# Two more slots for weight chunks and a coarser spread of the first norm's conditioning, in a hybrid decoder step

## The chip, the cores and the metric

The kernel runs on one core of one Trainium2 chip. The metric is the device time in microseconds (us) of one execution. The core has a matrix engine (TensorE, PE in the rows), VectorE (DVE), ScalarE (ACT), GpSimd (POOL) and SyncE (SP), whose queue issues nearly all loads from the chip's main memory (HBM). Each engine works through its own list of instructions in order. Where one needs another's result, it waits for a semaphore.

## The reference, cut to what matters

One decoder layer is computed for 256 prompt tokens and 8 x 4 sample tokens, 288 columns in all, in float32. Every norm is modulated by a conditioning vector `c` (one for the prompt, one for each of 8 samples).

```python
mod = silu(c) @ w_ada + b_ada                       # 2048 -> 6 * 2048
sh1, sc1, g1, sh2, sc2, g2 = split(mod, 6)
h = rmsnorm(x, norm1) * (1 + sc1) + sh1             # first norm, conditioned
proj = h @ w_in                                     # pool, z, x/B/C, dt
...                                                 # pooling mixer, Mamba-2 mixer
x = x + g1 * (mix @ w_out)
h2 = rmsnorm(x, norm2) * (1 + sc2) + sh2
...                                                 # gated MLP with a causal convolution
x = x + g2 * (act @ w_down)
```

The change touches how `sh1` and `sc1`, the conditioning of the first norm, are computed beside `h @ w_in`.

## The kernel before

Every activation lies with features on the 128 partitions and the 288 tokens along the row. A weight chunk is 128 x 1024 floats (512 KB). It is loaded by SP into a slot with the tag `raw`, and `split` (lines 214 to 219) makes two float32r parts of it: a copy on ACT (`whi`) and the rest on DVE (`wlo`). The activation is split likewise (`h1h`, `h1l`). `mm3` (lines 221 to 225) then issues three matmuls of 288 columns for each 128 x 128 tile: high x high, high x low, low x high. These make up the main stream of PE, from the input projection (`xbc`, `mm_uz`) over `mm_out` to `mm_gate`, `mm_val` and `mm_down`.

The conditioning is another kind of matmul. `ada_mm` (lines 249 to 254) puts the 9 conditioning vectors, padded to 32 columns, on PE as the stationary side and streams plain float32 weight columns. Four such matmuls, one for each 32 columns of the array, stand side by side; we call four that belong together a quad. The profile writes each of these matmuls as two records. `ada_group_units(gi)` makes `sh1` and `sc1` for one group of feature tiles. `KGROUPS` divides the 16 feature tiles into groups of 1, 1, 2, 4, 4 and 4. `ada_part_units` makes the other four parts of `mod` later, as `adap2` to `adap5`.

The input projection starts before all conditioning is known. For each group `gi`, `xbc_units(gi)` goes over 28 output tiles (`ET` = 28), multiplies by the group's feature tiles alone and adds into `cvp`, `upp`, `ups` or `zy`. Beside it the loop at lines 846 to 870 steps a generator for the conditioning of the next group: one step per output tile from the tile number `NX[gi]` on. At tile 24 (`ET - 4`) the generator is drained, and `modulate` makes the next group's `h1h` and `h1l`. A step of a group of four loads one chunk, which holds one quad; a step of a group of two holds two quads. A step loads its chunk, then yields, and issues the matmuls at the next step. There are 16 steps of a group of four, 8 of the group of two.

The slots: the class `_W` hands out `RAW1` = 8 slots in turn in the first half of the kernel, and one more (`RAW2`) from the output projection on. SP's list is in order, so a load whose slot is not free holds up all loads behind it. GpSimd issues some small transfers itself (software DMA); their descriptors lie in a scratch area in SBUF.

The order of instructions on each engine is not that of the Python code alone. A scheduler places the instructions when the program is built, by program order and by when it believes operands to be ready. So a quad may be broken: one of its matmuls stands before some matmuls of the main stream, three behind.

Of the kernel before, what the change touches and what calls it, by code (L numbers as in the profile page):

```python
# [19 lines left out]
KT = D // P  # L20
# [15 lines left out]
ET = XT + len(UEARLY) + 3 * ZEARLY  # L36
EPS = 1e-6
WU = (14, 2, 2, 2, 6)
RAW1, RAW2 = 8, 1
SPLIT1, SPLIT2 = 2, 2  # L40
YK = 2
NX = (10, 1, 1, 1, 1)
AY = 2

RA1, RA2, RB1, RB2, RB3 = 0.5, 0.4, 1.0, 1.0, 1.0
# [86 lines left out]
def kernel(ctx: ExitStack, tc, ins, outs):  # L132
    nc = tc.nc
# [28 lines left out]
    ada = kp.tile([P, 6, KT, NC9], F32, name="ada")  # L162
# [45 lines left out]
    def load(key):  # L208
        off, cols = S.items[key]
        t = wp[0].tile([P, RAWC], F32, tag="raw", name="raw_" + "_".join(map(str, key)))  # L210
        nc.sync.dma_start(t[:, :cols], wflat[off:off + P * cols].rearrange("(p n) -> p n", p=P))
        return t
# [59 lines left out]
    def ada_group_units(gi):  # L272

        k0, gk = KGROUPS[gi]
        nj = min(2 * gk, 4)
        nb = 2 * gk * P // nj
        per = RAWC // (nj * nb)
        ps = pa.tile([P, 512], F32, tag="ada", name=f"adag{gi}")
        for q in range(KT // per):
            raw = load(("ada", gi, q))  # L280
            yield
            if gk == 1:

                for kk in range(0, per, 2):
                    k = q * per + kk
                    for j in range(4):
                        nc.tensor.matmul(ps[32 * j:32 * j + 32, :nb], sc_c[:, k + j // 2, :],
                                         raw[:, kk * 256 + j * P:kk * 256 + j * P + P],
                                         start=(k == 0), stop=(k == KT - 2), tile_position=(0, 32 * j))
                if gi == 0 and q < WU[3]:  # L290
                    warm_pe(WU[2], raw[:, 0:P])
                continue
            for kk in range(per):
                ada_mm(ps, raw, q * per + kk, kk * nj * nb, nb, range(nj))
        r = 32 * nj
        if gk == 1:
            asb = ada_sb(ps, nb, f"g{gi}")
            pt = aux(f"adat_g{gi}")
            nc.tensor.matmul(pt[:, :r], asb[:, :nb], early[:, K_S2:K_S2 + r], start=True, stop=True)
            if gi == 0:  # L300
                warm_pe(WU[4], asb[:, 0:P])
        else:
            pt = ada_tr(ada_sb(ps, nb, f"g{gi}", r), nb, f"g{gi}", r)
        for i in range(nb // P):

            o = ada[:, 0:2, k0:k0 + gk, :].rearrange("p a (b i) c -> p a b i c", b=nj // 2)[:, :, :, i, :]
            b = bada[:, 0:2, k0:k0 + gk].rearrange("p a (b i) -> p a b i", b=nj // 2)[:, :, :, i]
            src = pt[:, i * r:(i + 1) * r].rearrange("p (a b c) -> p a b c", a=2, b=nj // 2)[:, :, :, 0:NC9]
            nc.vector.tensor_tensor(o, src, b.unsqueeze(3).to_broadcast([P, 2, nj // 2, NC9]), ALU.add)
        ada_scale(0, 1, early[:, V_N1:V_N1 + KT], k0, gk)  # L310
# [535 lines left out]
    for gi in range(len(KGROUPS)):  # L846
        last = gi + 1 == len(KGROUPS)
        if last:
            hi, lo = split(load(("dt",)), 0, KT * NH, "dt")
            ps = pm.tile([P, 512], F32, tag="mm", name="mm_dt")  # L850
# [3 lines left out]
        else:  # L854
# [5 lines left out]
            k0, gk = KGROUPS[gi + 1]  # L860
        for i, m in enumerate(xbc_units(gi)):
            if not last:
                if i >= NX[gi]:
                    next(nxt, None)
                if i == ET - 4:
                    drain(nxt)
                    modulate(xav(k0, gk), rstd1, 0, 0, k0, gk, f"g{gi + 1}")
            else:
                pull(back, 0.5 if m < 20 else RB1) if m >= 9 else None
                pull(adas, RA1 / AY)  # L870

# [360 lines left out]

# [27 lines left out]
```

## Time and profile before

| what | us |
| --- | --- |
| device time, median of 3 runs | 1394.89 |
| the three runs | 1394.83, 1396.73, 1394.89 |
| device time of the profiled execution | 1395.98 |
| its span, first to last instruction | 1394.2 |
| PE busy | 1374.9 |
| DVE busy | 822.3 |
| ACT busy | 577.0 |
| POOL busy | 259.8 |

The profiled execution lies 1.1 us above the median, and 1.8 us of it lie outside the span. A busy PE is not a PE that does as much as it can: matmuls overlap in its pipeline, and the records last longer than the distance between their starts. Such a stream is better read by the distance from one start to the next.

### The profile page before, as it was taken

The page shows a single profiled execution, that of the slowest core. Times are in us where ns is not written, and L with a number is a line of the kernel's source. Part 1 is how long each engine was busy: PE and PEld are TensorE (multiplying, and loading weights), DVE is VectorE, ACT ScalarE, POOL GpSimd, SP SyncE. Part 2 cuts the span into 40 slices and gives each one's busy share as a digit, 9 for nine tenths or more (in the row PEclk, how much of TensorE's full clock was granted, in tenths as well). Part 3 has the DMA queues.
Part 4 walks back from the last instruction along what each step waited for, and adds up shares of the span by engine and source line. Part 5 has one row for each costly group of instructions (what it writes and reads, how often), then busy time and mean ns, then how long its engine had stood idle before and what let it go on. Part 6 is the DMA issues. An engine that isn't in the chain of part 4 may idle for free.

```text
span 1394.2 us, 26416 instructions
## 1 busy us (share of the span) xinstructions
PE 1374.9 (99%) x10565; PEld 1253.5 (90%) x10565; DVE 822.3 (59%) x1409; ACT 577.0 (41%) x925; POOL 259.8 (19%) x466
## 2 busy tenths in 40 slices
PE   8999999999999999999999999999999999999997
PEld 7777888776668998989999999999999999999997
DVE  3775666867465446845665445666664466666553
ACT  5322333466673334533443333444343344444452
POOL 0000000344332222211211000221220011122221
PEclk9999999999999999999999999999999999999999
DMA  8889886867869886688655555655555555555631
GB/s 339 313 318 316 294 287 248 338 248 289 321 228 354 319 313 244 215 287 296 210 185 181 164 172 181 207 184 186 176 180 169 180 190 189 192 188 193 194 118 68
DMA packets 97196, 323.20 MB, mean 232 GB/s; under 512 B 10737, under 2 KB 19889, under 8 KB 97073
## 3 DMA queue, kind: packets, MB, share of 16 engines
q1 hardware_dynamic: 93168, 310.63, 64.8%
q0 software_dynamic: 3184, 9.69, 2.0%
q8 instruction: 83, 1.36, 0.4%
q10 hardware_dynamic: 720, 1.19, 0.2%
q14 instruction: 41, 0.33, 0.1%
HBM read 309.78 MB, written 10.39 MB: 230 GB/s over the span
## 4 chain that ended last, share of the span: by engine, by line
PE 70%; DVE 1%; issue 0%; ACT 0%; POOL 0%; DVEq 0%; POOLq 0%; ACTq 0%
PE mm_down L223 7%; PE mm_down L225 7%; PE mm_down L224 7%; PE mm_gate L225 6%; PE mm_gate L223 6%; PE mm_val L224 6%; PE mm_gate L224 6%; PE mm_val L225 6%; PE mm_val L223 6%; PE mm_out L223 3%; PE mm_out L224 2%; PE mm_out L225 2%; PE adap L252 2%; PE mm_up L223 1%; PE mm_up L224 1%; PE mm_up L225 1%
## 5 line engine op out<-in xcount | busy, mean ns | idle before, releaser
L223 PE MATMUL mm_down<-ah,whi_down 128*128 128x288 f32 x688 | 203.7, 296 | 0.0
L225 PE MATMUL mm_down<-ah,wlo_down 128*128 128x288 f32 x688 | 203.5, 296 | 0.0
L224 PE MATMUL mm_down<-al,whi_down 128*128 128x288 f32 x688 | 203.3, 295 | 0.0
L225 PE MATMUL mm_gate<-h2h,wlo_gate 128*128 128x288 f32 x640 | 190.2, 297 | 0.0
L223 PE MATMUL mm_gate<-h2h,whi_gate 128*128 128x288 f32 x640 | 189.8, 297 | 0.0
L224 PE MATMUL mm_gate<-h2l,whi_gate 128*128 128x288 f32 x640 | 189.3, 296 | 0.0
L224 PE MATMUL mm_val<-h2l,whi_val 128*128 128x288 f32 x640 | 188.8, 295 | 0.0
L225 PE MATMUL mm_val<-h2h,wlo_val 128*128 128x288 f32 x640 | 188.5, 295 | 0.0
L223 PE MATMUL mm_val<-h2h,whi_val 128*128 128x288 f32 x640 | 188.0, 294 | 0.0
L218 DVE TENSOR_TENSOR wlo_gate<-raw_gate,whi_gate 128x1024 fp32r<-128x1024 f32 x80 | 98.4, 1232 | 140.5 <-ACT whi_gate L217 140.3
L218 DVE TENSOR_TENSOR wlo_down<-raw_down,whi_down 128x1024 fp32r<-128x1024 f32 x96 | 108.2, 1127 | 116.0 <-ACT whi_down L217 115.1
L217 ACT CAST whi_down<-raw_down 128x1024 fp32r<-128x1024 f32 x96 | 92.2, 961 | 168.8 <-PE mm_down L224 120.3
L217 ACT CAST whi_gate<-raw_gate 128x1024 fp32r<-128x1024 f32 x80 | 83.8, 1050 | 168.3 <-PE mm_gate L224 76.2
L223 PE MATMUL xbc<-h1h,whi_xbc 128*128 128x288 f32 x448 | 139.1, 312 | 2.4 <-ACT h1h L350 1.3
L217 ACT CAST whi_val<-raw_val 128x1024 fp32r<-128x1024 f32 x80 | 84.1, 1051 | 127.8 <-issue 101.0
L224 PE MATMUL xbc<-h1l,whi_xbc 128*128 128x288 f32 x448 | 132.2, 296 | 0.0
L225 PE MATMUL xbc<-h1h,wlo_xbc 128*128 128x288 f32 x448 | 130.5, 298 | 0.6 <-DVE wlo_xbc L218 0.5
L224 PEld LDWEIGHTS mm_down<-al,whi_down 128*128 128x128 f32 x688 | 129.7, 189 | 0.0
L225 PEld LDWEIGHTS mm_down<-ah,wlo_down 128*128 128x128 f32 x688 | 129.6, 188 | 0.0
L223 PEld LDWEIGHTS mm_down<-ah,whi_down 128*128 128x128 f32 x688 | 129.6, 188 | 0.0
L223 PEld LDWEIGHTS mm_gate<-h2h,whi_gate 128*128 128x128 f32 x640 | 120.4, 188 | 5.0 <-ACT ah L1025 4.2
L224 PEld LDWEIGHTS mm_gate<-h2l,whi_gate 128*128 128x128 f32 x640 | 120.6, 189 | 0.0
(321 smaller groups left out, 3043.1 us busy)
## 6 DMA issues: line engine op xcount, KB each, us to landing
raw_adap<-wflat SPq DMA_DIRECT2D x128, 512.0 KB, 4.9
raw_gate<-wflat SPq DMA_DIRECT2D x80, 512.0 KB, 3.7
raw_val<-wflat SPq DMA_DIRECT2D x80, 512.0 KB, 3.5
raw_ada<-wflat SPq DMA_DIRECT2D x64, 512.0 KB, 5.5
raw_xbc<-wflat SPq DMA_DIRECT2D x55, 512.0 KB, 5.9
raw_down<-wflat SPq DMA_DIRECT2D x48, 512.0 KB, 3.6
raw_out<-wflat SPq DMA_DIRECT2D x32, 512.0 KB, 7.0
raw_down<-wflat SPq DMA_DIRECT2D x32, 384.0 KB, 3.1
```

The lines of the kernel that those rows point to most:

```text
L217: nc.scalar.copy(hi[:, :n], raw[:, a:a + n])
L218: nc.vector.tensor_tensor(lo[:, :n], raw[:, a:a + n], hi[:, :n].bitcast(F32), ALU.subtract)
L223: nc.tensor.matmul(ps, whi[:, w], bh, start=first, stop=False)
L224: nc.tensor.matmul(ps, whi[:, w], bl, start=False, stop=False)
L225: nc.tensor.matmul(ps, wlo[:, w], bh, start=False, stop=last)
L252: nc.tensor.matmul(ps[32 * j:32 * j + 32, :nb], sc_c[:, k, :], raw[:, c:c + nb], start=(k == 0), stop=(k == KT - 1), tile_position=(0, 32 ...
```

## The change

Four edits:

- `RAW1` goes from 8 to 10: two more slots of 4 KB a partition for weight chunks.
- The scratch for software-DMA descriptors is set to 8192 bytes, half of the default, which makes room for the two slots.
- In the loop, the generator for a group of two or four is stepped at every third output tile (`AE` = 3) instead of at every one. For the second group of one nothing changes.
- In `ada_group_units`, a step of a group of four loads two chunks and issues two quads (`AG` = 2).

```diff
--- before.py
+++ after.py
@@ -36,10 +36,11 @@
 ET = XT + len(UEARLY) + 3 * ZEARLY
 EPS = 1e-6
 WU = (14, 2, 2, 2, 6)
-RAW1, RAW2 = 8, 1
+RAW1, RAW2 = 10, 1
 SPLIT1, SPLIT2 = 2, 2
 YK = 2
 NX = (10, 1, 1, 1, 1)
+AG, AE = 2, 3
 AY = 2
 
 RA1, RA2, RB1, RB2, RB3 = 0.5, 0.4, 1.0, 1.0, 1.0
@@ -276,10 +277,17 @@
         nb = 2 * gk * P // nj
         per = RAWC // (nj * nb)
         ps = pa.tile([P, 512], F32, tag="ada", name=f"adag{gi}")
-        for q in range(KT // per):
-            raw = load(("ada", gi, q))
+
+
+        at = AG if gk == 4 else 1
+        for q0 in range(0, KT // per, at):
+            raws = [load(("ada", gi, q)) for q in range(q0, q0 + at)]
             yield
-            if gk == 1:
+            for q, raw in zip(range(q0, q0 + at), raws):
+                if gk > 1:
+                    for kk in range(per):
+                        ada_mm(ps, raw, q * per + kk, kk * nj * nb, nb, range(nj))
+                    continue
 
                 for kk in range(0, per, 2):
                     k = q * per + kk
@@ -289,9 +297,6 @@
                                          start=(k == 0), stop=(k == KT - 2), tile_position=(0, 32 * j))
                 if gi == 0 and q < WU[3]:
                     warm_pe(WU[2], raw[:, 0:P])
-                continue
-            for kk in range(per):
-                ada_mm(ps, raw, q * per + kk, kk * nj * nb, nb, range(nj))
         r = 32 * nj
         if gk == 1:
             asb = ada_sb(ps, nb, f"g{gi}")
@@ -860,7 +865,7 @@
             k0, gk = KGROUPS[gi + 1]
         for i, m in enumerate(xbc_units(gi)):
             if not last:
-                if i >= NX[gi]:
+                if i >= NX[gi] and (gk == 1 or (i - NX[gi]) % AE == 0):
                     next(nxt, None)
                 if i == ET - 4:
                     drain(nxt)
@@ -1232,7 +1237,7 @@
 
 def kernel(**inputs):
     ins = _layout(inputs)
-    nc = _bacc.Bacc("TRN2", target_bir_lowering=False, num_devices=1)
+    nc = _bacc.Bacc("TRN2", target_bir_lowering=False, num_devices=1, dynamic_dma_scratch_size=8192)
     i = {n: nc.dram_tensor(n, a.shape, F32, kind="ExternalInput").ap() for n, a in ins.items()}
     o = {n: nc.dram_tensor(n, s, F32, kind="ExternalOutput").ap() for n, s in _OUTS.items()}
     with _tile.TileContext(nc) as tc:
```

The scheduler lays out the whole program anew. Three places show what becomes of the order. In the names, `adag2` and `adag4` are the accumulators of the conditioning of groups 2 and 4, `raw_ada_4_5` is chunk 5 for group 4, and `xbc3_10` is output tile 10 of the input projection with the features of group 3. The last number of a name is a buffer.

PE, in the projection with group 1, before. The conditioning of the group of two stands between output tiles, eight matmuls (two quads) at a time:

```order
L252 MATMUL adag2_534<-raw_ada_2_2_567,sc_c_79 32x128 x8
L223 MATMUL xbc1_5_585<-h1h1_172,whi_xbc1_0_518 128x288
L224 MATMUL xbc1_5_585<-h1l1_188,whi_xbc1_0_518 128x288
L225 MATMUL xbc1_5_585<-h1h1_172,wlo_xbc1_0_519 128x288
L252 MATMUL adag2_534<-raw_ada_2_3_583,sc_c_79 32x128 x8
L223 MATMUL xbc1_6_601<-h1h1_172,whi_xbc1_0_518 128x288
```

The same place after:

```order
L253 MATMUL adag2_534<-raw_ada_2_2_591,sc_c_79 32x128
L224 MATMUL xbc1_5_565<-h1h1_172,whi_xbc1_0_518 128x288
L225 MATMUL xbc1_5_565<-h1l1_188,whi_xbc1_0_518 128x288
L226 MATMUL xbc1_5_565<-h1h1_172,wlo_xbc1_0_519 128x288
L253 MATMUL adag2_534<-raw_ada_2_2_591,sc_c_79 32x128 x2
L224 MATMUL xbc1_6_571<-h1h1_172,whi_xbc1_0_518 128x288
L225 MATMUL xbc1_6_571<-h1l1_188,whi_xbc1_0_518 128x288
L226 MATMUL xbc1_6_571<-h1h1_172,wlo_xbc1_0_519 128x288
L253 MATMUL adag2_534<-raw_ada_2_2_591,sc_c_79 32x128 x2
L224 MATMUL xbc1_7_577<-h1h1_172,whi_xbc1_0_518 128x288
```

The eight matmuls of one chunk, which stood together, are now dealt out in runs of one, two, two and three, with an output tile between each.

PE, in the projection with group 3, before:

```order
L224 MATMUL xbc3_6_1349<-h1l7_194,whi_xbc3_3_1345 128x288
L225 MATMUL xbc3_6_1349<-h1h7_178,wlo_xbc3_3_1346 128x288
L252 MATMUL adag4_1244<-raw_ada_4_4_1341,sc_c_79 32x256 x4
L223 MATMUL xbc3_7_1370<-h1h4_175,whi_xbc3_3_1345 128x288
L224 MATMUL xbc3_7_1370<-h1l4_191,whi_xbc3_3_1345 128x288
L225 MATMUL xbc3_7_1370<-h1h4_175,wlo_xbc3_3_1346 128x288
```

The same chunk after:

```order
L225 MATMUL xbc3_10_1423<-h1l7_194,whi_xbc3_5_1419 128x288
L226 MATMUL xbc3_10_1423<-h1h7_178,wlo_xbc3_5_1420 128x288
L253 MATMUL adag4_1244<-raw_ada_4_4_1377,sc_c_79 32x256 x4
L253 MATMUL adag4_1244<-raw_ada_4_5_1379,sc_c_79 32x256 x4
L224 MATMUL xbc3_11_1450<-h1h4_175,whi_xbc3_5_1419 128x288
L225 MATMUL xbc3_11_1450<-h1l4_191,whi_xbc3_5_1419 128x288
L226 MATMUL xbc3_11_1450<-h1h4_175,wlo_xbc3_5_1420 128x288
```

Here the conditioning of a group of four stood alone between output tiles, one quad after each; now two quads stand together, after every third tile.

DVE, from the moment at which the conditioning of group 4 is known (`adat_g4`) to the modulated features of that group (`h1l8` and so on), before. It stands beside output tiles 18 to 20 of 28:

```order
L309 TENSOR_TENSOR ada_77<-adat_g4_1631,early_69 128x2x2x9 x2
L543 TENSOR_TENSOR cvp3_163<-cvp3_163,xbc3_18_1643 128x256
L267 SCALAR_TENSOR_TENSOR amul_78<-ada_77,early_69 128x36
L543 TENSOR_TENSOR cvp3_163<-cvp3_163,xbc3_18_1643 128x8x4
L342 TENSOR_SCALAR h_g4_1763<-h_g4_1763,amul_78,ada_77 128x256 x3
L543 TENSOR_TENSOR cvp3_163<-cvp3_163,xbc3_19_1658 128x256
L543 TENSOR_TENSOR cvp3_163<-cvp3_163,xbc3_19_1658 128x8x4
L342 TENSOR_SCALAR h_g4_1763<-h_g4_1763,amul_78,ada_77 128x256
L351 TENSOR_TENSOR h1l8_195<-h_g4_1763,h1h8_179 128x288
```

After. It stands beside output tiles 25 to 27 of 28, and `xbc4_0` is the first tile that uses these features:

```order
L314 TENSOR_TENSOR ada_77<-adat_g4_1757,early_69 128x2x2x9 x2
L268 SCALAR_TENSOR_TENSOR amul_78<-ada_77,early_69 128x36
L347 TENSOR_SCALAR h_g4_1763<-h_g4_1763,amul_78,ada_77 128x256 x4
L548 TENSOR_TENSOR zy1_208<-zy1_208,xbc3_25_1779 128x288
L356 TENSOR_TENSOR h1l8_195<-h_g4_1763,h1h8_179 128x288
L356 TENSOR_TENSOR h1l9_196<-h_g4_1763,h1h9_180 128x288
L356 TENSOR_TENSOR h1l10_197<-h_g4_1763,h1h10_181 128x288
L356 TENSOR_TENSOR h1l11_198<-h_g4_1763,h1h11_182 128x288
L548 TENSOR_TENSOR zy1_208<-zy1_208,xbc3_26_1799 128x288
L219 TENSOR_TENSOR wlo_xbc4_0_1840<-raw_xbc_4_0_1837,whi_xbc4_0_1839 128x1024
```

The chain started beside output tile 18 of 28 and now starts beside tile 25.

## Rows read from the trace of the kernel before

**Rows 1.** Page, part 1: busy us (share of the span) xinstructions, by engine.

```profile
PE 1374.9 (99%) x10565; PEld 1253.5 (90%) x10565; DVE 822.3 (59%) x1409; ACT 577.0 (41%) x925; POOL 259.8 (19%) x466
```

**Rows 2.** PE's waits, the two longest: us in total, times, longest.

```profile
PE mm_uz L225 <- DVE wlo_uz L218: 1.4, 1, 1.4
PE cse L682 <- DVE ada L327: 1.4, 1, 1.4
```

**Rows 3.** Timeline of PE (start, us, instruction, [idle before <- releaser]): two waits.

```profile
89.33 0.40 PE L225 MATMUL xbc<-h1h,wlo_xbc 128*128 128x288 f32 x1 [0.53 <-DVE wlo_xbc L218]
...
274.49 0.40 PE L223 MATMUL xbc<-h1h,whi_xbc 128*128 128x288 f32 x1 [0.93 <-ACT whi_xbc L217]
```

**Rows 4.** Waits of SP's queue: loads that waited for a slot behind conditioning.

```profile
SPq L211 <- PE adag L252: 75.0, 48, 5.5
```

**Rows 5.** Timeline of PE: one quad of a group of four, then the main stream.

```profile
107.37 0.29 PE L225 MATMUL xbc<-h1h,wlo_xbc 128*128 128x288 f32 x1
107.59 0.64 PE L252 MATMUL adag<-raw_ada,sc_c 128*32 128x256 f32 x8
...
108.40 0.30 PE L224 MATMUL xbc<-h1l,whi_xbc 128*128 128x288 f32 x1
108.53 0.29 PE L225 MATMUL xbc<-h1h,wlo_xbc 128*128 128x288 f32 x1
```

**Rows 6.** Timeline of PE: two quads in a row, group of four.

```profile
76.69 0.30 PE L225 MATMUL xbc<-h1h,wlo_xbc 128*128 128x288 f32 x1
76.92 1.07 PE L252 MATMUL adag<-raw_ada,sc_c 128*32 128x256 f32 x16
...
78.16 0.30 PE L224 MATMUL xbc<-h1l,whi_xbc 128*128 128x288 f32 x1
```

**Rows 7.** Timeline of PE: two quads of the group of two.

```profile
42.04 0.29 PE L225 MATMUL xbc<-h1h,wlo_xbc 128*128 128x288 f32 x1
42.27 0.64 PE L252 MATMUL adag<-raw_ada,sc_c 128*32 128x128 f32 x16
...
43.08 0.29 PE L224 MATMUL xbc<-h1l,whi_xbc 128*128 128x288 f32 x1
```

**Rows 8.** Timeline of PE: later parts, two quads, then a single matmul of one.

```profile
222.23 0.29 PE L225 MATMUL xbc<-h1h,wlo_xbc 128*128 128x288 f32 x1
222.45 1.92 PE L252 MATMUL adap<-raw_adap,sc_c 128*32 128x512 f32 x16
...
224.54 0.29 PE L224 MATMUL xbc<-h1l,whi_xbc 128*128 128x288 f32 x1
...
225.07 0.29 PE L224 MATMUL xbc<-h1l,whi_xbc 128*128 128x288 f32 x1
225.29 1.04 PE L252 MATMUL adap<-raw_adap,sc_c 128*32 128x512 f32 x2
...
226.51 0.29 PE L223 MATMUL xbc<-h1h,whi_xbc 128*128 128x288 f32 x1
```

**Rows 9.** Timelines of PE and DVE: from group 4's conditioning to its features.

```profile
137.31 0.38 PE L263 MATMUL adat_g<-early,asb_g 128*128 128x128 f32 x2
...
139.09 1.34 DVE L342 TENSOR_SCALAR h_g<-h_g,amul,ada 128x256 f32<-128x256 f32 x3
...
142.06 1.23 DVE L218 TENSOR_TENSOR wlo_xbc<-raw_xbc,whi_xbc 128x1024 fp32r<-128x1024 f32 x1 [0.42 <-ACT whi_xbc L217]
```

**Rows 10.** Timelines of DVE and POOL: modulation of groups 3 and 4.

```profile
94.84 1.56 DVE L351 TENSOR_TENSOR h1l<-h_g,h1h 128x288 fp32r<-128x288 f32 x4
...
88.19 1.36 POOL L347 TENSOR_TENSOR h_g<-h_g,amul 128x128 f32<-128x128 f32 x1 [37.26 <-DVE cvp L543]
...
139.19 0.58 POOL L347 TENSOR_TENSOR h_g<-h_g,amul 128x128 f32<-128x128 f32 x1 [48.08 <-DVE cvp L543]
```

**Rows 11.** POOL's software DMA: issues on its timeline; KB, us to landing.

```profile
870.58 2.01 POOL L1040 DMA_DIRECT2D sq<-sbx  x4 [2.59 <-DMA o_ssms<-hst]
sq<-sbx POOLq DMA_DIRECT2D x16, 64.0 KB, 4.1
```

## The prediction, made before the changed kernel had run

> **What bounds the kernel now.** First the page's first part: PE is busy for 1374.9 of 1394.2 us, DVE for 822.3, POOL for 259.8 [rows 1]. So the kernel can only become faster where PE does less or waits less. Second, what ended PE's waits: the two longest take 1.4 us each, and both are for DVE [rows 2]. Two more, in the input projection, are idle times of 0.53 us (for DVE's low half of a chunk) and 0.93 us (for ACT's high half) [rows 3]. No long wait of PE is for a load. SP, on the other hand, waited 75.0 us in 48 loads for a slot that conditioning still held [rows 4]; that is where ten slots help, but these waits are SP's, and PE pays for none of them. The first two edits therefore bring nothing on their own. They cost something only through what the scheduler makes of the order, and there I count.
>
> **The price of leaving the main stream.** Two neighbouring matmuls of the main stream start 0.13 us apart (108.40 and 108.53) [rows 5]. Around one quad of a group of four the distance is 108.40 − 107.37 = 1.03; two steps of the main stream are in it, so the quad cost 1.03 − 0.26 = 0.77 [rows 5]. Two quads in a row cost 78.16 − 76.69 − 0.26 = 1.21 [rows 6]. The difference, 0.44, is the quad itself; 0.77 − 0.44 = 0.33 is the departure: out of the main stream and back. For the group of two, two quads cost 43.08 − 42.04 − 0.26 = 0.78; less the departure 0.45, or 0.22 a quad [rows 7]. For the later parts two quads cost 224.54 − 222.23 − 0.26 = 2.05, so (2.05 − 0.33) / 2 = 0.86 a quad. One matmul alone of such a quad cost 226.51 − 225.07 − 0.26 = 1.18, which is 0.33 + 0.85 [rows 8]: a piece broken off costs as much as a whole quad, because the four run side by side. I count for each run of conditioning matmuls one departure, and one quad for each four begun.
>
> **The change, part by part.** The new order of PE gives the numbers.
>
> *Groups of four in pairs.* Before, the 16 quads of groups 4 and 5 stood mostly alone; now most stand in twos. Group 4 goes from 16 runs to 9, group 5 from 16 to 9, group 3 from 19 to 16: 17 departures fewer.
>
> *The group of two, dealt out.* Its chunks have only eight matmuls each, and the scheduler breaks them into pieces of two to five. Its runs go from 8 to 16, the quads begun from 17 to 21. Net of both, 68 runs of the first norm's conditioning become 59: −9 × 0.33 = −3.0. Quads begun: +4 × 0.22 = +0.9 for the group of two and +1 × 0.44 = +0.4 for the groups of four. Together −1.7 us.
>
> *Parts moved.* The diff does not name the later parts, but the scheduler lays them out anew: 48 runs become 53, 79 − 76 = 3 more quads are begun. +5 × 0.33 + 3 × 0.86 = +4.2. The low end is +1.7, if broken pieces overlapped their neighbours after all; Rows 8 speak against it, so I take 4.2. PE's work in sum: −1.7 + 4.2 = +2.5 us.
>
> There is a rule against counting in this way. A departure costs 0.33 us whatever is streamed in it [rows 5, 6]. The Trainium skill, page "TensorEngine Tiling (Array Packing)", section "Key Properties", says that a change of the tiling mode (not of the tile alone) drains the engine; the trace agrees that leaving costs something. By that rule by itself the number of departures would be the whole price; this is the third rival below.
>
> *Waits that go.* In the new order the low half that PE waited for at 89.33 stands earlier in DVE's list, and the high half of 274.49 stands ahead of the long ACT instruction that held it. The idle time counts from the recorded end of the last matmul; the records last 0.30, and 0.13 is the step, so 0.17 has to be added: 0.53 + 0.17 = 0.7 and 0.93 + 0.17 = 1.1 [rows 3, 5]. Together −1.8. The two waits of 1.4 [rows 2] stand between the same neighbours as before; I leave them.
>
> *Waits that come.* The last step of a generator now comes later, so the chain from conditioning to the next group's features starts close to that group. For group 4: from the PE matmul that makes `adat_g4` to the first modulation on DVE 139.09 − 137.31 = 1.8 us; four modulations at 1.34 / 3 each 1.8; two additions at about 0.4; four `h1l` 1.56; the first low half of `xbc4_0` 1.2 [rows 9, 10]. That makes 1.8 + 1.8 + 0.8 + 1.6 + 1.2 = 7.2, all in a row on DVE. PE in the same time has 36 steps of the main stream, 36 × 0.13 = 4.7, then five conditioning matmuls in one run, 0.33 + 2 × 0.44 = 1.2, and then needs that low half: 5.9. It waits 1.3. POOL's half of the modulation, which the high half on ACT needs, runs beside it. At the other three boundaries, PE has 22 to 33 steps and one or two runs; the same sum there ends near zero. Ends: 0, if the scheduler's distance is enough, and 0.8, if POOL's first multiplication takes 1.36 us as for group 3 and not 0.58 as for group 4 [rows 10]. I take the middle, 0.4 each. New waits: 1.3 + 3 × 0.4 = +2.5. Waiting on DVE there queues the additions of the output tiles behind the modulation; their PSUM buffers come free later, which is in the ends above.
>
> *Halved scratch.* It costs nothing as long as POOL's issues find room. The densest place is four issues in 2.01 us, each landing after 4.1 us [rows 11]. One bound is zero; the other is the fifth rival.
>
> **The sum** against the profiled execution's own time, 1395.98 (span 1394.2 and 1.8 around it): 1395.98 + 2.5 − 1.8 + 2.5 = 1399.2. That execution lies 1.1 above the median of the runs shown, so 1398.1.
>
> **Rivals.** *The chains fit.* DVE has slack, and the order was laid out to suit it. New waits 0: 1395.98 + 2.5 − 1.8 − 1.1 = 1395.6. For it: PE waits for little anywhere [rows 1, 2]. Against: the 7.2 us are a plain sum of rows.
>
> *PE gains, so faster.* If pieces overlap with their neighbours and the new layout also removes the two waits of 1.4 [rows 2]: −3.0 + 0.4 + 1.7 − 1.8 − 2.8 = −5.5, hence 1389.4. Against: the price of the broken piece [rows 8] and the unmoved neighbours.
>
> *Only departures count.* All runs of PE that leave the main stream go from 138 to 134. If pieces cost nothing besides: −4 × 0.33 = −1.3, with the same waits 1395.98 − 1.3 + 0.7 − 1.1 = 1394.3. That is no change.
>
> *Late at all four boundaries, slower.* POOL's two operations share each boundary with DVE's two-input subtractions. At 1.36 in place of 0.58, twice, each boundary is 1.6 later [rows 10]: 4 × 1.6 = 6.4 in place of 2.5. 1395.98 + 2.5 − 1.8 + 6.4 − 1.1 = 1402.0. It decides once POOL's half ends later than DVE's, which for group 3 it did.
>
> *The scratch fills.* If each of the four issues had to wait until the one before had landed, POOL would be held 3 × (4.1 − 0.5) = 10.8 us at each of four places [rows 11]. POOL also makes small copies for each feed-forward tile. PE is reached only beyond POOL's lead; half of it reaching PE gives 4 × 5.4 = 22, some 1420. The Trainium skill, page "DMA: Bandwidth & Descriptors", section "SWDGE vs HWDGE vs iDMA", says that the rings of these descriptors lie in a reserved part of SBUF; no run here shows how full it gets.
>
> **How the numbers follow.** About 0.2%, 2.8 us, is what a measurement of this kernel can tell from no change: 1392.1 to 1397.7. Forecast (1398.1, its own range 1396.3 to 1399.9) 0.38, of which 0.22 lie above the bound and 0.16 within. Chains fit 0.20, within. Only departures 0.12, within. Faster 0.12, of which 0.10 below the bound. Late everywhere 0.13 and scratch 0.05, above. So faster 0.10, same 0.16 + 0.20 + 0.12 + 0.02 = 0.50, slower 0.40. The range from 1393.5 to 1402.2 leaves out nearly all of the faster case and the scratch, and a tail of "late everywhere".
>
> **What the profile after would show.** If I am right: PE's departures around groups 4 and 5 cost 1.21 for two quads; the waits at 89 and 274 are gone; a wait of about 1.3 us for DVE's `wlo_xbc` stands at the start of the projection with group 4, and less than 0.8 at the other three; the parts have five more runs. The second rival shows in single part matmuls that cost 0.4 rather than 1.18; the fourth in POOL's modulation of 1.3 us and more at every boundary; the fifth in wide gaps between POOL's DMA issues. The prediction is wrong if PE waits for loads anywhere, or if the time after 420 us, where the order hardly changes, differs.

## The result and the profile after

The changed kernel takes 1399.81 us (median of 7 executions) against 1396.30 us for the kernel before on the same chip: +3.5 us, a ratio of 1.0028 with a 95% interval from 1.0016 to 1.0039. The prediction was 1398.1 against 1394.89, +3.2 us. The profiled execution took 1399.81 us, its span is 1398.0 us; before it was 1394.2, so the span grew by 3.8.

The first part of the page, against [rows 1]:

```profile
PE 1377.6 (99%) x10565; PEld 1256.8 (90%) x10565; DVE 824.5 (59%) x1409; ACT 577.0 (41%) x925; POOL 259.3 (19%) x466
```

PE's busy time grew by 2.7 us with the same number of instructions, so some seven tenths of the change are work or slower work of PE. The longest waits of PE (us in total, times, longest), against [rows 2]:

```profile
PE xbc L224 <- ACT h1h L355: 2.1, 2, 1.3
PE mm_uz L226 <- DVE wlo_uz L219: 1.8, 1, 1.8
PE cse L687 <- DVE ada L332: 1.5, 1, 1.5
PE xbc L224 <- DVE zy L548: 1.5, 1, 1.5
```

The 1.3 in the first row is an old wait at the start of the projection (1.3 before as well). The other 0.8 and the last row are new. On PE's timeline they are the first matmuls of the projections with groups 2 and 3:

```profile
63.45 0.53 PE L224 MATMUL xbc<-h1h,whi_xbc 128*128 128x288 f32 x2 [0.79 <-ACT h1h L355]
...
101.01 0.37 PE L224 MATMUL xbc<-h1h,whi_xbc 128*128 128x288 f32 x1 [1.47 <-DVE zy L548]
```

The two waits of [rows 3] are gone. A pair of quads costs what the prediction used, 115.11 − 113.65 − 0.26 = 1.20 us, against 1.21 in [rows 6]:

```profile
113.65 0.29 PE L226 MATMUL xbc<-h1h,wlo_xbc 128*128 128x288 f32 x1
113.87 1.07 PE L253 MATMUL adag<-raw_ada,sc_c 128*32 128x256 f32 x16
...
115.11 0.29 PE L225 MATMUL xbc<-h1l,whi_xbc 128*128 128x288 f32 x1
```

**Where the 3.8 us lie.** The whole stream of PE can be divided up. We take each distance between two neighbouring starts of the main stream, subtract the undisturbed step of 0.132 us, and add up what is left by what stands between the two (and on the step behind it), from the first instruction to the second tile of the output projection. Behind that the two kernels run nearly alike: from the 97th matmul of the output projection to the end both take 964.0 us.

| excess over the main stream, us | before | after | difference |
| --- | --- | --- | --- |
| conditioning of group 2 | 6.4 | 9.9 | +3.6 |
| conditioning of group 3, with the new wait at 63 | 15.3 | 15.6 | +0.3 |
| conditioning of group 4, with the new wait at 101 | 12.6 | 11.4 | −1.2 |
| conditioning of group 5 | 12.2 | 10.3 | −1.9 |
| later parts and the small matmuls (before: with the wait at 274) | 97.1 | 99.7 | +2.6 |
| waits inside the main stream (before: the one at 89, three small delays) | 1.7 | 0.0 | −1.7 |
| from the first of the two pauses near 314 to 12 us behind it | 15.4 | 17.6 | +2.2 |
| the rest | 6.1 | 6.1 | 0.0 |
| sum | 166.9 | 170.6 | +3.8 |

The line of the two pauses was not in the prediction. The windows there (length, busy us by engine, granted PE clock, DMA share, GB/s) show it. Before:

```profile
316.00:318.00 2.00, 1.09 (x4) 1.12 (x5) 2.00 (x8) 1.99 (x5) 0.01 (x1) 0.71 0.88 338
318.00:320.00 2.00, 2.00 (x11) 1.66 (x11) 2.00 (x8) 1.98 (x6) 0.37 (x1) 0.50 1.06 392
320.00:322.00 2.00, 2.00 (x13) 1.57 (x12) 1.03 (x2) 1.21 (x5) 1.64 (x3) 0.94 1.07 383
```

After:

```profile
316.00:318.00 2.00, 0.93 (x5) 0.70 (x5) 2.00 (x5) 1.98 (x5) 0.97 (x2) 0.93 0.64 193
318.00:320.00 2.00, 1.41 (x5) 1.22 (x5) 2.00 (x9) 1.98 (x6) 0.00 (x0) 0.50 0.99 342
320.00:322.00 2.00, 2.00 (x11) 1.88 (x11) 1.97 (x6) 1.99 (x7) 0.07 (x1) 0.50 1.06 392
322.00:324.00 2.00, 2.00 (x10) 2.00 (x9) 0.01 (x1) 0.43 (x1) 0.66 (x1) 0.50 0.64 228
324.00:326.00 2.00, 2.00 (x16) 0.83 (x17) 0.00 (x0) 0.00 (x0) 0.00 (x0) 0.86 0.00 0
```

The second pause of each kernel, before and after, and two steps of the main stream behind it:

```profile
316.91 0.58 PE L682 MATMUL cse<-csr,selr 128*128 128x288 f32 x1 [1.42 <-DVE ada L327]
...
318.59 0.58 PE L687 MATMUL cse<-csr,selr 128*128 128x288 f32 x1 [1.52 <-DVE ada L332]
...
319.21 0.44 PE L225 MATMUL mm_uz<-h1l,whi_uz 128*128 128x288 f32 x1
319.45 0.44 PE L226 MATMUL mm_uz<-h1h,wlo_uz 128*128 128x288 f32 x1
```

At the two pauses (1.4 and 1.4 us before, 1.8 and 1.5 after) the granted clock falls to 0.50, 1.2 GHz, the lower of its two levels. A window of 2 us at 0.71 has 2 × 0.29 / 0.5 = 1.2 us of it, so the clock fell at 316.8 before, as the second pause ended. After, with 0.3 us of it in the window from 316, it fell at 317.7, when 0.9 us of the second pause were still to come. Added up in this way the low stretch lasts 3.4 us before and 6.8 us after. At that level a step of the main stream takes 0.24 us instead of 0.13. Of the +2.2 us, the pauses themselves are 0.5; the other 1.7 are half of the 3.4 us by which the stretch at half clock is longer.

### The profile page after: what moved, and what is told of

Its sections match the earlier page's. It is cut to its first block, busy times and chain, and to the rows that moved or that the text cites. A ratio compares the mean times of both kernels' runs of the same rounds, so it can differ in the third digit from the quotient of the medians.

```text
span 1398.0 us, 26442 instructions
## 1 busy us (share of the span) xinstructions
PE 1377.6 (99%) x10565; PEld 1256.8 (90%) x10565; DVE 824.5 (59%) x1409; ACT 577.0 (41%) x925; POOL 259.3 (19%) x466
## 4 chain that ended last, share of the span: by engine, by line
PE 70%; DVE 1%; issue 0%; ACT 0%; POOL 0%; DVEq 0%; POOLq 0%; ACTq 0%
PE mm_down L224 7%; PE mm_down L226 7%; PE mm_down L225 7%; PE mm_gate L226 6%; PE mm_gate L224 6%; PE mm_val L225 6%; PE mm_gate L225 6%; PE mm_val L226 6%; PE mm_val L224 6%; PE mm_out L224 2%; PE mm_out L225 2%; PE mm_out L226 2%; PE adap L253 2%; PE mm_up L224 1%; PE mm_up L225 1%; PE mm_up L226 1%
```

## The experiments

The theory at the start: PE is the bound, and what the change costs is departures from the main stream (the group of two dealt out, the parts broken) and waits at the group boundaries. The rivals: the slots and loads matter, the scratch costs, or the low clock near 320 us is the whole of it. All ratios are against the kernel before on the same chip. A ratio is formed from all executions, so it need not be the quotient of the two medians. Where its interval holds 1, the median alone shows no change.

| kernel | median us | before us | ratio, 95% interval |
| --- | --- | --- | --- |
| x1_slots | 1397.14 | 1396.34 | 1.0009, 1.0000 to 1.0017 |
| x2_eight | 1397.55 | 1396.34 | 1.0006, 0.9997 to 1.0015 |
| x3_two_every | 1395.04 | 1396.34 | 0.9992, 0.9984 to 1.0001 |
| x4_fours | 1393.03 | 1396.34 | 0.9977, 0.9968 to 0.9986 |
| x5_fours8 | 1397.00 | 1396.82 | 1.0005, 0.9993 to 1.0017 |
| x6_taps | 1399.36 | 1396.82 | 1.0011, 1.0000 to 1.0021 |
| x7_scratch | 1397.06 | 1396.82 | 0.9998, 0.9989 to 1.0008 |
| x8_every_second | 1400.74 | 1396.82 | 1.0031, 1.0019 to 1.0043 |
| x9_mix | 1388.77 | 1396.41 | 0.9941, 0.9927 to 0.9955 |
| x10_mix22 | 1389.92 | 1396.41 | 0.9951, 0.9937 to 0.9965 |
| x11_only_two | 1397.35 | 1396.41 | 1.0002, 0.9993 to 1.0011 |
| x12_mix8 | 1393.88 | 1396.20 | 0.9981, 0.9970 to 0.9992 |

### The edits apart: slots, scratch, spread

**x1_slots**, on the kernel before:

```diff
-RAW1, RAW2 = 8, 1
+RAW1, RAW2 = 10, 1
-    nc = _bacc.Bacc("TRN2", target_bir_lowering=False, num_devices=1)
+    nc = _bacc.Bacc("TRN2", target_bir_lowering=False, num_devices=1, dynamic_dma_scratch_size=8192)
```

> The kernel before with ten weight slots and the halved scratch alone; the conditioning is stepped as before. Theory (PE's departures are the price): the order of the first norm's conditioning stays as before, the later parts go from 48 runs to 50 and begin one quad more, 2 x 0.33 + 0.86 = +1.5 us, so about 1397.8; no new wait at a group boundary, and the two waits that went in the changed kernel (at 88.5 and 274) stay. Rival (the loads matter): SP's 75 us of waits for slots fall to less than half and PE gains from it, faster than before by 2 us or more. Rival (halved scratch costs): gaps between POOL's DMA issues, 10 us and more slower.

Measured +0.8 us. The slots bring nothing: SP's waits for slots behind the conditioning stay (75.0 us in [rows 4]):

```profile
SPq L211 <- PE adag L252: 73.2, 49, 5.5
```

The wait at 274 (1.1 us), which was expected to stay, is gone; the one at 88.5 stays. What the slots cost, 0.8 us by the medians, is an accident of the order. Of PE's excess, the stretch at the two pauses grows by 2.1 us and the small waits inside the stream shrink by 0.6. The first pause is longer because the low half that PE waits for takes longer on DVE. In x1_slots it is this row, and POOL's second operation on `hf`, an addition, runs beside it:

```profile
311.63 2.01 DVE L218 TENSOR_TENSOR wlo_uz<-raw_uz,whi_uz 128x1024 fp32r<-128x1024 f32 x1
...
311.44 1.13 POOL L654 TENSOR_TENSOR hf<-hf,s 128x384 f32<-128x384 f32 x1
```

In the kernel before the same low half begins 0.7 us after that addition has ended, and takes 1.21 us:

```profile
311.42 1.14 POOL L654 TENSOR_TENSOR hf<-hf,s 128x384 f32<-128x384 f32 x1
...
313.29 1.21 DVE L218 TENSOR_TENSOR wlo_uz<-raw_uz,whi_uz 128x1024 fp32r<-128x1024 f32 x1
```

The Trainium skill, page "SBUF — State Buffer", section "Who interferes with whom", says that a DVE instruction with two inputs in SBUF contends with a GpSimd instruction that reads SBUF. These rows agree: 2.01 against 1.21 us. It goes with the slots in all 13 traces that have the pause: in the six kernels with eight slots the low half takes 1.21 us and the first pause is 1.4, in the seven with ten slots it takes 2.0 and the pause is 1.8 (x6_taps, below, has no pause there).

**x7_scratch**, the second of the two edits alone.

> The kernel before with the halved scratch alone; the order of the instructions on PE is that of before. Theory: POOL's issues are far enough apart, no change (within 0.5 us of the kernel before), and the software-DMA landings are those of before (4.1 us for sq). Rival (the scratch fills): landings or issue gaps of POOL longer by some us, 5 us and more slower.

Measured 0.9998 with an interval from 0.9989 to 1.0008, and `sq` lands after 4.2 us against 4.1 in [rows 11]. The halved scratch costs nothing that can be measured; the fifth rival falls.

**x2_eight**, the changed kernel with the edits of x1_slots undone.

> The changed kernel with eight slots and the full scratch: only the stepping of the conditioning is changed. Theory: the conditioning's order is that of the changed kernel (50 runs for groups 2 to 5, 76 quads), the waits at the starts of groups 2 and 3 stay (about 1.0 and 1.5 us), and the parts lose 3 runs and 2 quads against the changed kernel, 3 x 0.33 + 2 x 0.86 = 2.7 us: about 1397.1. Rival (the ten slots are what makes pairs possible): with eight slots PE waits for loads or SP's waits grow, and the time is above 1400.

Measured 1397.55, as the theory had it. Both new waits stay (0.79 and 1.48 us on PE's timeline), and PE does not wait for loads. By the medians the spread alone costs 1.2 of the 3.5 us and the slots alone 0.8, but the two intervals reach down to no change, so this split, and the 1.5 us that would come only with both, are not shown by the times. What the order shows is that the parts have 50 runs and 77 quads with either of them, and 53 runs and 79 quads with the two together.

**x11_only_two**, the kernel before with the loop's new rule for the group of two alone:

```diff
-                if i >= NX[gi]:
+                if i >= NX[gi] and (gk != 2 or (i - NX[gi]) % AE == 0):
```

> The kernel before with one edit: the group of two is stepped at every third output tile instead of every one. Eight slots, full scratch, groups of four as before. Theory: the group of two goes from 8 runs and 17 quads to 16 and 21, 8 x 0.33 + 4 x 0.22 = +3.5; group 3 loses 4 runs and 3 quads, -2.6, of which the low half at 88.5 is freed, -0.7; and a wait of 1.0 us comes at the start of group 2: +1.2 us, about 1397.8 against 1396.5. Rival (spreading is cheap, the groups of four are the cost): within 0.3 us of the kernel before or faster.

Measured +0.9 us, of the expected size, but the interval holds no change as well. The excess of PE tells more: conditioning of group 2 6.4 to 10.0 (+3.6), of group 3 15.3 to 12.8 (−2.5). Two terms of the expectation failed and made up for each other: the low half at 89 is still waited for (0.53 us), and no wait comes at the start of group 2, though this group is dealt out as in the changed kernel. In the changed kernel ACT copied a high half first and then made `h1h`:

```profile
62.02 1.04 ACT L218 CAST whi_xbc<-raw_xbc 128x1024 fp32r<-128x1024 f32 x1 [2.84 <-PE xbc L225]
62.98 0.76 ACT L355 CAST h1h<-h_g 128x288 fp32r<-128x288 f32 x2
```

In x11_only_two it did so the other way round:

```profile
62.06 0.77 ACT L355 CAST h1h<-h_g 128x288 fp32r<-128x288 f32 x2 [2.97 <-POOL h_g L353]
62.73 1.05 ACT L218 CAST whi_xbc<-raw_xbc 128x1024 fp32r<-128x1024 f32 x1
```

So the changed kernel's wait of 0.8 us at group 2 is one for ACT's order.

**x3_two_every**, the changed kernel without that part:

```diff
-                if i >= NX[gi] and (gk == 1 or (i - NX[gi]) % AE == 0):
+                if i >= NX[gi] and (gk <= 2 or (i - NX[gi]) % AE == 0):
```

> The changed kernel, but the group of two is stepped at every output tile again, as before; only groups of four are spread at every third tile, in pairs. Theory: the group of two has 8 runs and 17 quads again in place of 16 and 21, group 3 one run and two quads fewer: 9 x 0.33 + 4 x 0.22 + 2 x 0.44 = -4.7 us, and the wait of 1.0 us at the start of group 2 goes, while that of 1.5 us at group 3 stays: 1399.8 - 5.7 = 1394.1. Rival (slots, scratch or the clock around 320 us are the cause, not the spread of the group of two): 1399.8 within 1.

Measured 1395.04, 4.8 us less than the changed kernel, where 5.7 were expected. Conditioning of group 2 costs 6.4 again, of group 3 13.6 instead of 15.6, and the wait at the start of group 2 is gone. So dealing out the group of two is the costliest part of the change as it stands, and the rival that has the cause elsewhere falls. It is not that dear by itself: in x11_only_two group 3 gave back 2.5 us of it.

### The distance of the chain: x8_every_second

```diff
-AG, AE = 2, 3
+AG, AE = 2, 2
```

> The changed kernel with a step at every second output tile instead of every third; pairs and ten slots stay. The generators end by tile 15 instead of 24, so the chain to the next group's features has 72 and 110 steps of the main stream ahead of groups 3 and 4 in place of 21 and 32, and 36 in place of 24 ahead of group 2. Theory: the wait of 1.5 us at the start of group 3 goes, that of 1.0 at group 2 goes or shrinks; the conditioning's runs cost the same (49 against 50 runs, 3 quads more, -0.1), the parts 2.7 less: 1399.8 - 1.5 - 0.5 - 2.7 = 1395.1. Rival (distance to the group is not what makes these waits): they stay, 1397.

Wrong by over 5 us: 1400.74, no faster than the changed kernel (ratios 1.0031 and 1.0028, with intervals that overlap). The waits at the starts of groups 2 and 3 do go, as the theory had it, but others take their place in the middle of the projections. The chain of group 2 now stands beside tile 16, and on DVE's list the modulation stands ahead of a low half that PE needs at once:

```profile
56.82 0.81 PE L226 MATMUL xbc<-h1h,wlo_xbc 128*128 128x288 f32 x3 [0.73 <-DVE wlo_xbc L219]
```

Three waits between 53 and 57 us (0.38, 0.62 and 0.73 us, this the longest) come before a low clock, a fourth of 0.41 us just behind its fall at 57.2. The windows there:

```profile
56.00:58.00 2.00, 0.90 (x4) 0.46 (x3) 2.00 (x5) 0.77 (x2) 0.92 (x1) 0.79 0.82 270
58.00:60.00 2.00, 1.96 (x5) 0.92 (x5) 1.27 (x6) 0.00 (x0) 0.00 (x0) 0.50 0.85 317
...
62.00:64.00 2.00, 2.00 (x11) 0.92 (x10) 0.84 (x3) 0.00 (x0) 0.00 (x0) 0.50 0.02 6
```

Two more low stretches follow, at 95 and 323 us. Between 50 and 350 us the clock is low for 13.7 us in this trace and for 6.8 in the changed kernel's, and half of the 6.8 us between them, 3.4 us, is time. (The traced execution, 1403.06, lies 2.3 us above the median.) So more distance does remove these two waits, but that does not make the kernel faster. What counts is also whether something that PE needs soon stands behind the chain in DVE's list.

### Pause and clock: x6_taps

```diff
-            for i in range(1, 4):
+            for i in range(1, 2 if g == 2 else 4):
```

> The changed kernel without 10 of the 15 multiply-adds that VectorE does for the second-last but one quarter (group 2) of the Mamba convolution: part of the convolution is left out. They stand ahead of the low half that PE waits for at 314 us. Theory (the pause costs twice: itself, and the low clock behind it): the waits of 1.8 and 1.5 us at 314 to 319 go and the granted clock stays 1.00 in that stretch, -3.3 and -1.6 to -2.0: 1394.7. Rival (the low clock comes from what stands in that stretch, not from the pause): the waits go, the clock still falls, 1396.5. Rival (the time is paid elsewhere): 1399 and more.

This kernel leaves out 10 of the 15 multiply-adds of one quarter of the convolution. The stretch behaves as the theory says: no pause of more than a quarter us, and the clock stays up. The windows:

```profile
316.00:320.00 4.00, 3.76 (x28) 3.12 (x27) 1.56 (x7) 3.97 (x12) 3.19 (x6) 1.00 1.01 372
320.00:324.00 4.00, 4.00 (x36) 1.99 (x34) 1.73 (x3) 3.97 (x8) 0.21 (x1) 1.00 0.38 140
...
244.00:248.00 4.00, 4.00 (x21) 3.33 (x21) 3.47 (x8) 2.56 (x8) 0.69 (x2) 0.73 0.08 29
```

PE's excess there falls from 17.6 to 12.2 us. But the time of the traced execution does not follow (1400.61; the median is 1399.36). A new wait comes at 341 us for the low half of a later tile, with a low clock of its own behind it, and the clock also falls at 244 us:

```profile
PE mm_uz L226 <- DVE wlo_uz L219: 2.1, 1, 2.1
```

The second rival, by which the time is paid elsewhere, holds for this execution. It does not hold for all: of the 12 executions three, with a mean granted clock of 0.998, took 1396.0 to 1396.5 us, two at 0.996 took 1397.8 and 1397.9, and seven at 0.995 took 1399.1 to 1400.6. All seven of the changed kernel took 1399.3 or more. So where the mean clock stayed up, time did come back; why it does in some executions only, no run shows. The window at 244 us shows something else: PE is busy for all of 4.00 us, and yet the clock falls, behind a row of small matmuls (24 to 192 columns) from 241 us on. What PE did before the clock fell was thus a pause in one place, and small work without a pause in the other. The same small matmuls stand in the changed kernel's trace at 241 to 245 us, at a granted clock of 1.00 and with no fall behind them.

### Fewer departures: x4, x5, x9, x10, x12

If departures are the price, fewer of them must help. **x4_fours** steps the group of two as before and gives the groups of four four quads at a time, on top of x3_two_every:

```diff
-AG, AE = 2, 3
+AG, AE = 4, 4
```

> Ten slots and halved scratch; the group of two at every tile as before; the groups of four in fours (four chunks, four quads in a row) at every fourth output tile, so that the generator is done by tile 13. Theory: against the changed kernel 15 departures of the conditioning fewer and small changes of the quads, -5.9 us by my prices; the parts have 3 runs and 2 quads fewer, -2.7; no wait at the starts of groups 2 and 3, -2.5: 1399.8 - 11.1 = 1388.7, or 1391 if the two waits of before (1.8 together) come back. Rival (a burst of four loads in a row makes PE wait for loads): waits of PE behind raw chunks, and 1395 or more.

Measured 1393.03: faster than both kernels, but by less than expected. The conditioning of groups 4 and 5 costs 19.0 us of excess (21.7 in the changed kernel, 24.9 before). Group 3 gives part of it back. As in x8, its chain ends in the middle of a projection, and a low half stands behind three modulations on DVE:

```profile
84.85 1.33 DVE L347 TENSOR_SCALAR h_g<-h_g,amul,ada 128x256 f32<-128x256 f32 x3
86.10 1.21 DVE L219 TENSOR_TENSOR wlo_xbc<-raw_xbc,whi_xbc 128x1024 fp32r<-128x1024 f32 x1
...
87.36 0.40 PE L226 MATMUL xbc<-h1h,wlo_xbc 128*128 128x288 f32 x1 [1.55 <-DVE wlo_xbc L219]
```

**x9_mix** therefore keeps group 3 in pairs at every third tile, and gives fours at every fourth to groups 4 and 5 alone:

```diff
-        at = AG if gk == 4 else 1
+        at = (AG if gi == 3 else 4) if gk == 4 else 1
-                if i >= NX[gi] and (gk == 1 or (i - NX[gi]) % AE == 0):
+                if i >= NX[gi] and (gk <= 2 or (i - NX[gi]) % (AE if gi == 2 else 4) == 0):
```

> Ten slots and halved scratch; the group of two at every tile as before; group 3 in pairs at every third tile as in the changed kernel; groups 4 and 5 in fours at every fourth. Theory: x4_fours lost 3.4 us in waits at 84 to 89 us, because the chain of group 3 then stands in the middle of the projection ahead of a low half that PE needs at once; with group 3 as in x3_two_every there is instead the one wait of 1.5 us at 98 us. Conditioning runs cost 37.9 us by my prices against 39.5 in x4_fours, so 1393.0 - 1.6 - 2 = 1389.5. Rival (fours cost elsewhere, as loads that come late): 1393 or more.

Measured 1388.77, 7.6 us less than the kernel before and 11 less than the changed kernel, within 1 us of the expectation. The conditioning of groups 2 to 5 costs 39.9 us of excess against 46.5 before. Its page and its longest new waits:

```profile
PE 1366.0 (98%) x10565; PEld 1255.0 (90%) x10565; DVE 823.6 (59%) x1409; ACT 576.9 (42%) x925; POOL 256.2 (18%) x466
```

```profile
PE xbc L224 <- ACT whi_xbc L218: 1.3, 1, 1.3
PE xbc L224 <- DVE zy L548: 1.0, 1, 1.0
```

PE is busy for 1366.0 us, 8.9 less than in [rows 1], with the same instructions.

**x10_mix22** starts group 3's chain two tiles earlier still:

```diff
-                if i == ET - 4:
+                if i == (ET - 6 if gi == 2 else ET - 4):
```

> x9_mix, and the generator of group 3 is drained at tile 22 instead of 24, so its chain begins two tiles earlier and PE has 26 steps of the main stream instead of 21, and the additions of the last three output tiles still stand behind the modulation on VectorE. Theory (the wait of 1.5 us at the start of group 3 is VectorE's modulation standing ahead of the additions that free PSUM): two tiles are 1.6 us, so most of that wait goes, one more quad and one more run cost 0.8: within 1 us of x9_mix, the wait below 0.8. Rival: the wait moves into the projection with group 2, to a low half behind the modulation, as in x4_fours: 1 to 2 us slower than x9_mix.

Measured 1389.92, 1.2 us more than x9_mix by the medians, but the two intervals overlap, so it is not shown to be slower. The wait at the start of group 3 shrinks from 1.04 to 0.55 us of idle time, below 0.8 as the theory had it, and 1.0 us of delay (by the distances between PE's starts) stands in the projection with group 2 instead, as the rival had it. Moving the chain moved a part of the wait and gained nothing that can be measured.

**x5_fours8** and **x12_mix8** are x4_fours and x9_mix with eight slots and the full scratch.

> The kernel of x4_fours with eight slots and the full scratch. Theory: the conditioning is as in x4_fours; the parts have the 48 runs and 76 quads of the kernel before, 2 x 0.33 + 0.86 = 1.5 us less than x4_fours, and the low half that PE waits for at 313 takes about 1.2 us again instead of 2.0, so the wait there is 1.4 instead of 1.8 us and the low clock after it about 1 us of time shorter; the waits of x4_fours at 84 to 89 us (3.4 in all) stay: 1393.0 - 1.5 - 1.0 = 1390.5. Rival (a burst of four loads needs ten slots): PE waits for loads, 1394 and more.

> x9_mix with eight slots and the full scratch. Theory (ten slots are needed for bursts of four loads): as in x5_fours8 the chunks of the main stream come late behind the burst, PE waits some 2.5 to 3.5 us more for the high and low halves between 100 and 200 us, against 1.5 us less for the parts and some 0.5 to 1 us less low clock at 313 us: 1388.8 + 1 = 1390. Rival (fours run as well with eight slots): the parts' 1.5 and 0.8 of the conditioning are gained, 1386.5.

Both are slower than with ten slots, x5 by 4.0 us and x12 by 5.1. For x5_fours8 the rival was right, a burst of four needs ten slots; x12_mix8 took that as its theory, and its size was too small. In x12 PE waits for a high half of a chunk that has not landed, once for 3.2 us, and the clock falls near the end of that wait (at 163.8 us, for 6.8 us):

```profile
PE xbc L224 <- ACT whi_xbc L218: 4.1, 2, 3.2
```

ACT's waits for such chunks (us, times, longest) in x12_mix8:

```profile
ACT whi_xbc L218 <- DMA raw_xbc<-wflat: 54.3, 13, 11.1
```

and in x9_mix:

```profile
ACT whi_xbc L218 <- DMA raw_xbc<-wflat: 21.8, 5, 8.9
```

So the two slots of the change do have a use: they carry bursts of four loads, which the change does not have. Since x7_scratch shows that the scratch costs nothing, it is the slots that make these differences.

## Why the prediction was right, point by point

The direction, the size (+3.2 against +3.5) and the range were right. Not every step was, and that the sum came this near is in part luck, as the terms below show.

**Price of departures: right.** The conditioning of group 5, which has no wait near it, went from 12.2 to 10.3: −1.9 where 7 runs less and one quad more give −7 × 0.33 + 0.44 = −1.9. Group 2 went up by 3.6 where 8 × 0.33 + 4 × 0.22 = 3.5 was counted. Group 3 and group 4 hold a new wait each; by the counted runs they would have changed by −0.6 and −2.8, and they changed by +0.3 and −1.2, so the waits are 0.9 and 1.5 to 1.6, as the idle times of 0.79 and 1.47 say with the prediction's 0.17 added to each. Without them all conditioning changed by −1.6, where −1.7 was predicted.

**Parts: right in kind, somewhat too high.** The line of the table is +2.6; with the wait at 274 (1.1) that was in it before, the parts and what stands beside them cost 3.7 more, against 4.2. The upper price, a broken piece costs as much as a quad, was the one to take. The third rival (only the number of departures counts) gave −1.3 for PE's work; measured are −1.6 + 3.7 = +2.1, and the pieces are the difference. The Trainium skill, page "TensorEngine Tiling (Array Packing)", section "Key Properties", says no more than that a change of the tiling mode (not of the tile alone) drains the engine. The trace agrees that leaving has a price of its own: taken from one quad and from two in a row, it is 0.33 to 0.35 us for quads of 128, 256 and 512 columns alike. The second rival, by which single matmuls of the parts cost 0.4, falls by the changed kernel's trace: by PE's starts they cost 1.17 to 1.18 us each, a whole quad alone 1.20.

**Waits that go: right,** −1.8, and three small delays of 0.3 to 0.4 us went besides.

**Waits that come: right sum, wrong place.** Predicted were 2.5: 1.3 at group 4 and 0.4 at each of the others. Measured are 2.3 of idle time (2.6 with 0.17 added to each): 0.8 at group 2, 1.5 at group 3, none at 4 and 5. The one at group 2 is for ACT's `h1h` behind a high half (above), an order that the prediction did not look at. At group 4 the chain ran like this, on PE, DVE, DVE and PE:

```profile
149.68 0.38 PE L264 MATMUL adat_g<-early,asb_g 128*128 128x128 f32 x2
...
150.66 1.66 DVE L347 TENSOR_SCALAR h_g<-h_g,amul,ada 128x256 f32<-128x256 f32 x4
...
154.45 1.21 DVE L219 TENSOR_TENSOR wlo_xbc<-raw_xbc,whi_xbc 128x1024 fp32r<-128x1024 f32 x1
...
156.01 0.40 PE L226 MATMUL xbc<-h1h,wlo_xbc 128*128 128x288 f32 x1
```

The first modulation began 1.0 us after the matmul and not 1.8 as in [rows 9], where DVE had another addition to do in between. The low half was ready at 155.7, 6.0 us after the matmul instead of 7.2, and PE came to it after 6.3. At group 3 the step that failed is the bound: the prediction named the additions behind the modulation and took them to be within 0.8. DVE did them last:

```profile
97.42 1.61 DVE L347 TENSOR_SCALAR h_g<-h_g,amul,ada 128x256 f32<-128x256 f32 x4
98.95 1.55 DVE L356 TENSOR_TENSOR h1l<-h_g,h1h 128x288 fp32r<-128x288 f32 x4
100.43 1.17 DVE L548 TENSOR_TENSOR zy<-zy,xbc 128x288 f32<-128x288 f32 x3
```

PE's first matmul of group 3 waited for the first of these three, with DVE's 3.0 us of modulation ahead of it. It was not POOL's first multiplication, which ended at 97.4, before the last modulations. The fourth rival, a slow POOL at every boundary, falls too: its first multiplication took 1.28 us at group 3 alone, 0.30 at group 2 and 0.58 at groups 4 and 5.

**The two waits of 1.4: wrong to leave.** The neighbours on PE were the same, but the first grew to 1.8: on DVE the low half took 2.01 us from 314.07 on, beside POOL's addition, as in x1_slots. With the low clock behind them the stretch cost 2.2 us more. x1_slots, which has the long stretch too, lies only 0.8 us above the kernel before, and x3_two_every, which has it as well, 1.3 below; so this is not the whole of the change. The total came out near the forecast because the small waits (−1.0) and the parts (−0.5) were off the other way; that is the luck.

**The clock that is left.** The kernel before alone, executed 95 times beside these experiments on three chips, has a median of 1394.8 us where its mean granted clock was 0.998 (10 times), 1396.2 at 0.996 (36 times), 1397.5 at 0.995 (19 times) and 1400.6 at 0.992 (4 times). The changed kernel lies at 1399.4 at 0.995 (4 of 7), 1.9 us above the kernel before at the same mean clock; its single executions at 0.994 and 0.996 lie 3.4 and 3.6 above. So at the same mean clock the change costs 1.9 to 3.6 us (an estimate from few executions, where 0.001 of clock goes with about 1 us), and what is left of the 3.5 us, if anything, is that its mean clock is more often lower. Which of its stretches brings that down in each execution stays open, since only one execution of each kernel has a trace.

## What to carry to other kernels

Where PE is full, count what makes it leave its main stream, and count pieces: one matmul broken off from four that run side by side costs as much as all four (0.33 us of departure and a whole quad). Spreading small work evenly is dear (+3.6 us of excess for the group of two), bundling is cheap, as long as the slots carry the burst (x9_mix with ten slots 1388.8, x12_mix8 with eight 1393.9). And before a chain of VectorE is moved, look at what stands behind it in VectorE's list, and at what stands ahead of its last link on ScalarE: at group 3, in x4_fours and in x8_every_second PE waited for the first, at group 2 for the second.

## What was not expected of the hardware

A pause of PE can cost twice. The granted clock fell to 0.50 at the two pauses near 314 us in all 13 traces that have them, after three waits of 0.4 to 0.7 us and at one of 1.6 us in x8_every_second, and in the wait of 3.2 us in x12_mix8. It did not fall at the wait of 1.5 us at 101 us in the changed kernel. It also fell with PE busy all the time, behind small matmuls (x6_taps at 244 us).

The length of the low stretch was not a function of the pause alone: between 50 and 350 us it was either 3.4 or 6.8 us in every trace. With two pauses of 1.4 us it was 3.4 in five kernels, but 6.8 in x2_eight (below); with pauses of 1.8 and 1.5 us it was 6.8 in five, but 3.4 in x8_every_second and x9_mix. What went with it in all 13 was where in the second pause the clock fell. In the six with 6.8 us, 0.5 to 1.5 us of that pause were still to come (0.9 in the changed kernel, 1.2 in x2_eight, whose clock fell at 316.7 and whose pause ended at 318.0). In the seven with 3.4 us it was over, or, as in the kernel before, within 0.1 us of its end. Pauses of the same length thus cost 1.7 us more or less. Why the clock falls where it does is open. The windows of x2_eight:

```profile
316.00:318.00 2.00, 0.58 (x6) 0.38 (x4) 2.00 (x8) 1.98 (x4) 0.72 (x1) 0.68 0.57 199
318.00:320.00 2.00, 2.00 (x10) 1.66 (x11) 2.00 (x6) 1.98 (x6) 0.00 (x0) 0.50 1.00 365
320.00:322.00 2.00, 2.00 (x9) 2.00 (x10) 1.39 (x5) 1.99 (x7) 1.23 (x2) 0.50 0.93 321
322.00:324.00 2.00, 2.00 (x9) 1.55 (x8) 0.71 (x1) 0.25 (x1) 0.77 (x2) 0.61 1.06 382
```
